# A two-layer hybrid attention backbone on one core: the whole program in one scheduling block, ordered by the timeline machine

## The chip, the cores and the metric

The kernel runs on one core of one Trainium2 chip. The metric is device time in microseconds (us) of that core, from the start of the launch to its end. Three runs of the kernel before took 3088.96 us in the median, between 3088.78 and 3089.18.

## The reference: what is computed

1024 latent tokens and 256 context tokens of width 1024 pass through two layers. Each layer normalizes the tokens, applies a shift and a scale computed from a conditioning vector (adaLN), projects them to many heads with one wide weight matrix, mixes them, projects back and adds the result to the tokens. Cut to what matters here:

```
h = rmsnorm(x, g_pre[l]) * (1.0 + scale) + shift          # also for the context tokens
layer 0:  s = q k^T / 8 ; p = softmax(s)                  # 8 heads, two maps per head
          a = p[0] - lam * p[1] ; oa = rmsnorm(a v) ; ua = oa * silu(gate)
          ub = bb * short_conv(bc * bh) * silu(bg)         # 8 groups of 128 channels
layer 1:  16 heads of 2-D neighbourhood attention (NA) plus dense attention to the context
          4 heads of gated linear attention (GLA), forward and backward
x = x + gate * rmsnorm(u @ w_out[l], g_post[l])
```

All is float32; every product of two matrices is computed as three passes over values split in a high and a low part.

## The kernel before, in words

TensorE (PE) is given nearly all the work that counts. A projection is cut into units: one 1024 x 128 block of a weight matrix is loaded (`wraw`), split into `whi` by ScalarE (ACT, L243) and `wlo` by GpSimd (POOL, L244), and multiplied with the tokens `hA`/`hB` in three chunks of 512, 512 and 256 tokens. One chunk is 24 matmuls into one tile `pj` in PSUM (L437); there are two such tiles (`ps_pj`, bufs=2). Whatever reads a `pj` tile sets when the next chunk but one may start.

Layer 0 goes head by head (`diff_head`, L563). A head has ten steps of 128 query rows (`units`, L640): eight against all 1280 keys, the last two (context queries) against 256 keys. A step computes scores into the single PSUM tile `S` (L589) for map 1, then map 0; VectorE (DVE) takes the row maximum (L591), ACT the exponential `p` (L593), DVE joins the two maps (L599), PE transposes the result (`atr`, L611), ACT and DVE split it into `ath` and `atl` (L614, L615), and after every second step PE multiplies it with the values (`av`, L625). At the end of a head ACT squares the result (L628), PE sums it (`ms`, L635, in the same PSUM slot as `S`), ACT takes logarithm and exponential for the reciprocal root (L309, L310, each with a table load), DVE refines it with three operations (L311 to L313) and multiplies (L637).

Between these dependent steps the program runs projection units of other heads and of the convolution as filler: `ws.run(n)` asks for n more units of the list in `units0`, `ws.until` for all up to a name. The keys of a head go through `rope` (L511), which copies a `pj` tile with ACT (L516) into a buffer of the pool tag `p0`. That tag has two buffers, which the probabilities `p0`, the reciprocal root `rs` and the `ropex` tiles share.

Layer 1 runs GLA heads and then eight pairs of NA heads (`na`, L1403) in the same manner: scores `NS` (L1435, two halves of one PSUM tile), bias and minimum on DVE (L1439), exponential on ACT, scaling on POOL (L1443), transposes `ntr` (L1484), a split into `pth` and `ptl` by ACT and DVE (L1493, L1494), and the product with the values `nav` (L1461). Projections `pj` of the next pair are the filler.

The order of the instructions on each engine comes from the tile framework's scheduler. It takes the program as traced, with its dependencies and priorities, and fixes the queue of every engine before the launch; on the chip each engine runs its queue strictly in that order and waits where an operand isn't ready. Before, the program stands in no block, and the default machine orders it. The last stage (L909) is a `manual_schedule` block, written in its final order.

Of the kernel before, what the change touches and what calls it, by code (L numbers as in the profile page):

```python
# [40 lines left out]
class Stream:  # L41
# [39 lines left out]
    def run(self, n):  # L81
        for _ in range(n):
            if not self.step():
                return
# [15 lines left out]
class Kernel:  # L100
# [6 lines left out]
        return (ctx or self.ctx).enter_context(self.tc.tile_pool(name=name, bufs=bufs, **kw))  # L107

    def run(self):
        self.setup()  # L110
        with ExitStack() as es:
            self.hp = self.pool("hp", ctx=es)
            rope_es, out_es = ExitStack(), ExitStack()
            self.start(rope_es)
            conv_es = self.layer0(rope_es)
            self.layer1(self.out0(conv_es, out_es), out_es)
            with ExitStack() as es2:
                self.out1(es2)
# [1493 lines left out]
```

## Time and profile before

| what | value |
|---|---|
| median of 3 runs | 3088.96 us |
| the profiled execution | 3089.97 us |
| its span | 3087.9 us |
| PE busy | 2935.2 us, 95% |
| DVE, ACT, POOL busy | 1910.7, 1503.5, 1027.9 us |
| mean granted TensorE clock | 0.991 |

Outside the span lie 2.1 us of the profiled execution. PE is idle for 152.7 us of the span; the stretches in which it idles are found with the table of windows, and what it waits for with the list of waits. A row of the waits gives who waited for whom, the us in total, the times and the longest. A row of the timeline gives the start, the time, the engine, the line, and what is written from what; brackets at its end give the idle time before it and who ended it.

### The profile page before, as it was taken

The page shows a single profiled execution, that of the slowest core. Times are in us where ns is not written, and L with a number is a line of the kernel's source. Part 1 is how long each engine was busy: PE and PEld are TensorE (multiplying, and loading weights), DVE is VectorE, ACT ScalarE, POOL GpSimd, SP SyncE. Part 2 cuts the span into 40 slices and gives each one's busy share as a digit, 9 for nine tenths or more (in the row PEclk, how much of TensorE's full clock was granted, in tenths as well). Part 3 has the DMA queues.
Part 4 walks back from the last instruction along what each step waited for, and adds up shares of the span by engine and source line. Part 5 has one row for each costly group of instructions (what it writes and reads, how often), then busy time and mean ns, then how long its engine had stood idle before and what let it go on. Part 6 is the DMA issues. An engine that isn't in the chain of part 4 may idle for free. (4 is left out here: it accounts for less than half of the span.)

```text
span 3087.9 us, 42515 instructions
## 1 busy us (share of the span) xinstructions
PE 2935.2 (95%) x16244; PEld 2439.3 (79%) x16244; DVE 1910.7 (62%) x3272; ACT 1503.5 (49%) x2761; POOL 1027.9 (33%) x813
## 2 busy tenths in 40 slices
PE   6999999999999999999999898989899999999898
PEld 4888888888888887888877777777778888887686
DVE  5675757575665757564244778685836666667723
ACT  4554535353544445453344555555535555556522
POOL 3212131313021211205233334342435555556622
PEclk9999999999999999999999999999999999999999
DMA  6111110211110211115342112111131111113323
GB/s 227 35 45 48 49 52 28 65 35 58 35 59 28 65 35 48 45 42 208 109 150 76 45 39 69 55 43 58 55 95 36 47 44 44 43 44 99 118 76 123
DMA packets 236982, 206.59 MB, mean 67 GB/s; under 512 B 43591, under 2 KB 194538, under 8 KB 236778
## 3 DMA queue, kind: packets, MB, share of 16 engines
q1 hardware_dynamic: 236778, 203.87, 21.2%
q8 instruction: 128, 2.10, 0.3%
q14 instruction: 76, 0.62, 0.1%
HBM read 168.17 MB, written 35.67 MB: 66 GB/s over the span
## 5 line engine op out<-in xcount | busy, mean ns | idle before, releaser
L244 POOL TENSOR_TENSOR wlo<-wraw,whi 128x1024 fp32r<-128x1024 f32 x149 | 367.0, 2463 | 1097.3 <-ACT whi L243 1017.0
L437 PE MATMUL pj<-hBh,whi 128*128 128x512 f32 (+1 forms) x1712 | 383.3, 353 | 6.2 <-ACT hBh L355 4.8
L437 PE MATMUL pj<-hBl,whi 128*128 128x512 f32 (+1 forms) x1712 | 369.1, 347 | 0.9 <-DVE hBl L356 0.9
L437 PE MATMUL pj<-hBh,wlo 128*128 128x512 f32 (+1 forms) x1712 | 352.1, 344 | 0.0
L243 ACT CAST whi<-wraw 128x1024 fp32r<-128x1024 f32 x176 | 184.5, 1048 | 321.3 <-PE ops L753 193.7
L437 PEld LDWEIGHTS pj<-hBl,whi 128*128 128x128 f32 x1712 | 278.0, 191 | 35.9 <-DVE hBl L356 1.1
L437 PEld LDWEIGHTS pj<-hBh,wlo 128*128 128x128 f32 x1712 | 277.2, 190 | 36.8
L437 PEld LDWEIGHTS pj<-hBh,whi 128*128 128x128 f32 x1712 | 273.2, 190 | 40.8 <-ACT hBh L355 5.4
L437 PE MATMUL pj<-hAh,whi 128*128 128x512 f32 x968 | 280.5, 410 | 14.6 <-ACT ropex L516 13.0
L437 PE MATMUL pj<-hAl,whi 128*128 128x512 f32 x968 | 255.4, 395 | 0.0
L591 DVE TENSOR_REDUCE st<-S 128x1 f32<-128x1280 f32 (+1 forms) x160 | 203.9, 1274 | 79.2 <-PE S L589 79.2
L437 PE MATMUL pj<-hAh,wlo 128*128 128x512 f32 x968 | 249.9, 393 | 0.0
L1443 POOL TENSOR_TENSOR np<-np,nst 128x640 f32<-128x640 f32 x128 | 166.5, 1304 | 193.1 <-DVE nst L1442 161.0
L593 ACT ACTIVATE p<-S,st 128x1280 f32<-128x1280 f32 (+1 forms) x160 | 186.1, 1163 | 81.9 <-DVE st L591 80.4
L437 PEld LDWEIGHTS pj<-hAh,wlo 128*128 128x128 f32 x968 | 180.2, 188 | 36.3
L437 PEld LDWEIGHTS pj<-hAh,whi 128*128 128x128 f32 x968 | 170.2, 191 | 48.1 <-ACT ropex L516 14.4
L437 PEld LDWEIGHTS pj<-hAl,whi 128*128 128x128 f32 x968 | 178.7, 190 | 34.8
L589 PE MATMUL S<-kst,qd 128*128 128x512 f32 (+1 forms) x832 | 192.1, 360 | 0.3 <-ACT p L593 0.2
L589 PEld LDWEIGHTS S<-kst,qd 128*128 128x128 f32 x832 | 137.2, 188 | 39.9 <-ACT p L593 21.3
L1439 DVE CUSTOM_DVE_ANT_0 np<-NS,nB 128x640 f32<-128x640 f32 x128 | 105.3, 823 | 91.2 <-PE NS L1436 85.5
L614 ACT CAST ath<-atr 128x512 fp32r<-128x512 f32 (+1 forms) x208 | 99.1, 505 | 113.4 <-PE atr L611 112.8
L1494 DVE TENSOR_TENSOR ptl<-ntr,pth 128x512 fp32r<-128x512 f32 (+2 forms) x224 | 117.6, 536 | 49.0 <-ACT pth L1493 45.2
(361 smaller groups left out, 6276.8 us busy)
## 6 DMA issues: line engine op xcount, KB each, us to landing
wraw<-in_ev_w_in_dram SPq DMA_DIRECT2D x64, 512.0 KB, 4.0
wraw<-in_od_w_in_dram SPq DMA_DIRECT2D x56, 512.0 KB, 3.6
wraw<-in_w_out_dram SPq DMA_DIRECT2D x55, 512.0 KB, 3.7
wraw<-in_w_mod_dram SPq DMA_DIRECT2D x48, 512.0 KB, 3.8
sgT<-gt SPq DMA_DIRECT2D x32, 256.0 KB, 2.0
uT<-sg SPq DMA_DIRECT2D x8, 640.0 KB, 4.3
nG<-in_rpbp_dram SPq DMA_DIRECT2D x128, 40.0 KB, 2.3
xt<-in_x_dram SPq DMA_DIRECT2D x8, 512.0 KB, 6.2
```

The costliest lines, as they stand in the source:

```text
L243: nc.scalar.copy(out=hi, in_=u.raw)
L244: (nc.vector if u.lo_eng == "v" else nc.gpsimd).tensor_tensor(out=lo, in0=u.raw, in1=hi.bitcast(F32), op=ALU.subtract)
L437: nc.tensor.matmul(ps[:, 0:tn], lhsT=a[:, k, :], rhs=self.h_at(k, t0, tn)[b], start=n == 0, stop=n == 23)
L589: nc.tensor.matmul(S[:, c0:c0 + tn], lhsT=qd[:, 2 * m + part, P * qt:P * qt + P], rhs=self.kst[m][:, t0:t0 + tn], start=part == 0, stop=pa ...
L591: nc.vector.tensor_reduce(out=st[:, m:m + 1], in_=S[:, 0:n], axis=AX.X, op=ALU.max, negate=True)
L593: nc.scalar.activation(out=p[m][:, 0:n], in_=S[:, 0:n], func=AF.Exp, bias=st[:, m:m + 1], accum_out=st[:, 2 + m:3 + m])
L614: nc.scalar.copy(out=dh, in_=tv)
L1439: nc.vector.tensor_tensor_reduce(out=p, in0=S[:, z0:z0 + 640], in1=bias[2 * i + m][:, c0:c0 + 640], scale=1.0, scalar=3e38, op0=ALU.add, o ...
L1443: nc.gpsimd.tensor_tensor(out=p, in0=p, in1=st[:, 2:3].broadcast_to([P, 640]), op=ALU.mult)
L1494: nc.vector.tensor_tensor(out=lv[:, s:e], in0=tr[:, s:e], in1=hv[:, s:e].bitcast(F32), op=ALU.subtract)
```

## The change

`run` now opens one block around the whole program and asks for the timeline machine; the old body of `run` becomes `work`.

```diff
     def run(self):
+        with self.tc.block(schedule_with_timeline_sim=True):
+            self.work()
+
+    def work(self):
         self.setup()
         with ExitStack() as es:
             self.hp = self.pool("hp", ctx=es)
```

The instructions themselves, their operands and their buffers stay. In the changed file line numbers are higher by 4 and the numbers in names by 1 (S_3147 is S_3148 there). On PE 15726 instructions, on DVE 3242, on ACT 2387, on POOL 818 and on SP 618 are put in an order; the same ones stand in both. The last stage keeps its order.

**The end of a head, on PE.** This is the second head of layer 0, from the last score step against all keys (S_3147) into the two steps of the context queries (S_3214, S_3223). Before:

```order
L589 MATMUL S_3147<-kst0_2106,qd_3004 128x256
L437 MATMUL pj_3180<-hBh_156,wlo_3057 128x512 x7
L437 MATMUL pj_3250<-hBh_156,whi_3056 128x256 x8
L437 MATMUL pj_3250<-hBl_157,whi_3056 128x256 x5
L589 MATMUL S_3214<-kst1_2107,qd_3206 128x256 x2
L437 MATMUL pj_3250<-hBl_157,whi_3056 128x256 x3
L437 MATMUL pj_3250<-hBh_156,wlo_3057 128x256 x8
L271 MATMUL modps_3278<-wraw_2997,sst_804 32x256
L611 MATMUL atr_3231<-ident_73,p0_3155 128x128 x4
L611 MATMUL atr_3238<-ident_73,p0_3155 128x128 x2
L589 MATMUL S_3223<-kst0_2106,qd_3206 128x256 x2
```

and now:

```order
L593 MATMUL S_3148<-kst0_2107,qd_3005 128x256
L593 MATMUL S_3215<-kst1_2108,qd_3207 128x256 x2
L615 MATMUL atr_3232<-ident_74,p0_3156 128x128 x4
L615 MATMUL atr_3239<-ident_74,p0_3156 128x128 x4
L593 MATMUL S_3224<-kst0_2107,qd_3207 128x256 x2
L629 MATMUL av_3284<-ath_3160,vh_2318 128x256
L615 MATMUL atr_3246<-ident_74,p0_3156 128x128 x2
L629 MATMUL av_3284<-atl_3161,vh_2318 128x256
```

The 31 `pj` matmuls that stood between the scores of S_3147 and the transposes of the next step are gone from here, and so are those behind them up to `ms`; they now stand earlier in the head, between the score steps of the other queries. The same holds at the end of all eight heads.

**The boundary between two heads, on ACT.** From the last square of the second head to the first copies of keys of the third. Before:

```order
L628 ACTIVATE qf_2218<-av_3346 128x256
L309 ACT_TABLE_LOAD
L309 ACTIVATE rt_3360<-ms_3355,eps_80 128x1280
L214 ACT_TABLE_LOAD
L214 ACTIVATE csg_3415<-pj_3386 128x512
L310 ACTIVATE rs_3359<-rt_3360 128x1280
L214 ACTIVATE csg_3445<-pj_3420 128x512
L243 CAST whi_3480<-wraw_3372 128x1024
L214 ACTIVATE csg_3475<-pj_3450 128x256
L516 COPY ropex_3513<-pj_3486 128x512
L529 CAST ropex_3513<-ropex_3513 128x512
L516 COPY ropex_3549<-pj_3524 128x512
```

and now:

```order
L632 ACTIVATE qf_2219<-av_3347 128x256
L313 ACT_TABLE_LOAD
L313 ACTIVATE rt_3361<-ms_3356,eps_81 128x1280
L314 ACT_TABLE_LOAD
L314 ACTIVATE rs_3360<-rt_3361 128x1280
L520 COPY ropex_3514<-pj_3487 128x512
L247 CAST whi_3593<-wraw_3385 128x1024
L533 CAST ropex_3514<-ropex_3514 128x512
L520 COPY ropex_3550<-pj_3525 128x512
L520 COPY ropex_3586<-pj_3561 128x256
```

Before, three silu operations on `pj` tiles of the convolution stood among and behind the table loads, and the first `ropex` copy came after them; now that copy follows the exponential directly.

**The same boundary, on PE.** From the last `ms` to the third head's keys (pj_3486, pj_3524 and pj_3560 are its three chunks; pj_3598 is the first chunk of its queries). Before:

```order
L635 MATMUL ms_3355<-qf_2218,onesD_78 128x256
L437 MATMUL pj_3386<-hAh_154,wlo_3369 128x512 x8
L290 MATMUL modtr_3411<-sel_84,modrow_3378 128x2 x2
L437 MATMUL pj_3420<-hBh_156,whi_3368 128x512 x8
L437 MATMUL pj_3420<-hBl_157,whi_3368 128x512 x8
L437 MATMUL pj_3420<-hBh_156,wlo_3369 128x512 x8
L437 MATMUL pj_3450<-hBh_156,whi_3368 128x256 x8
L437 MATMUL pj_3450<-hBl_157,whi_3368 128x256 x8
L437 MATMUL pj_3450<-hBh_156,wlo_3369 128x256 x8
```

and now:

```order
L639 MATMUL ms_3356<-qf_2219,onesD_79 128x256
L441 MATMUL pj_3561<-hBh_157,whi_3381 128x256 x8
L441 MATMUL pj_3561<-hBl_158,whi_3381 128x256 x8
L441 MATMUL pj_3561<-hBh_157,wlo_3382 128x256 x8
L441 MATMUL pj_3599<-hAh_155,whi_3481 128x512 x8
L441 MATMUL pj_3599<-hAl_156,whi_3481 128x512 x8
```

Before, the convolution's chunks pj_3386, pj_3420 and pj_3450 and then all three key chunks followed `ms`. Now the first two key chunks (pj_3487 and pj_3525) stand ahead of `ms`, and the third follows it at once. All seven boundaries of layer 0 look like this, and the end of the eighth head has no `pj` behind `ms` either: projections back (`ops`) follow.

**A stretch of NA, on PE.** The middle of the second pair of heads; `nqd` is a step's query tile, and a step's scores are two half steps of four `NS` matmuls (two lines of 384 and 256 columns, each twice). Before:

```order
L1484 MATMUL ntr_20935<-ident_73,np_20789 128x128
L1484 MATMUL ntr_20935<-ident_73,np_20799 128x128
L437 MATMUL pj_20946<-hBh_12808,whi_20527 128x512 x5
L1461 MATMUL nav_19409<-pth_20911,nv_20054 128x256 x2
L1461 MATMUL nav_19409<-ptl_20912,nv_20054 128x256 x2
L1461 MATMUL nav_19409<-pth_20927,nv_20054 128x256 x2
L1461 MATMUL nav_19409<-ptl_20928,nv_20054 128x256 x2
L437 MATMUL pj_20946<-hBh_12808,whi_20527 128x512 x3
L437 MATMUL pj_20946<-hBl_12809,whi_20527 128x512 x8
L437 MATMUL pj_20946<-hBh_12808,wlo_20528 128x512 x8
L1435 MATMUL NS_19408<-nk1_19747,nqd_20986 128x384
L1436 MATMUL NS_19408<-nk1_19747,nqd_20986 128x256
```

and now:

```order
L1440 MATMUL NS_19409<-nk0_19747,nqd_20781 128x256
L1465 MATMUL nav_19410<-ptl_20743,nv_20055 128x256 x2
L1488 MATMUL ntr_20821<-ident_74,np_20693 128x128
L1488 MATMUL ntr_20821<-ident_74,np_20703 128x128
L1439 MATMUL NS_19409<-nk1_19748,nqd_20883 128x384
L1440 MATMUL NS_19409<-nk1_19748,nqd_20883 128x256
L1439 MATMUL NS_19409<-nk1_19748,nqd_20883 128x384
L1440 MATMUL NS_19409<-nk1_19748,nqd_20883 128x256
L1488 MATMUL ntr_20836<-ident_74,np_20693 128x128
L1488 MATMUL ntr_20836<-ident_74,np_20703 128x128
L1488 MATMUL ntr_20836<-ident_74,np_20693 128x128
L1488 MATMUL ntr_20836<-ident_74,np_20703 128x128
```

Before, `pj` matmuls (5 to 30 of them) stood behind every half step or every second one throughout. Now seven half steps, from the first of nqd_20781 to the first of nqd_21096, follow each other with transposes and values alone between them, and longer runs of up to 43 `pj` matmuls stand in the rest of the pair. There is one such stretch of seven in each of the eight pairs.

**At the start, on SP.** The loads of the last seven blocks of modulation weights (of 16) and of `rowsB` have moved back: 22 loads of 512 KB stood ahead of `rowsB`, now 33 do, among them the rest of `x`, the context, cos and sin and the first projection weights.

**In GLA, on PE.** The projections between the first and the last `gl` matmul (L1137) of a head fall from 36.1 us to 31.7 us in the second to fourth head, and rise from 33.0 to 36.3 us in the first (the matmuls counted in the orders, at about 0.22 us for 512 columns and 0.12 us for 256, as they follow each other in the trace).

## Rows read from the trace of the kernel before

**Rows 1.** The page, span and busy time by engine.

```profile
span 3087.9 us, 42515 instructions
...
PE 2935.2 (95%) x16244; PEld 2439.3 (79%) x16244; DVE 1910.7 (62%) x3272; ACT 1503.5 (49%) x2761; POOL 1027.9 (33%) x813
```

**Rows 2.** Windows of four stages: busy time of each engine.

```profile
core 0: us, PE busy (x) PEld busy (x) DVE busy (x) ACT busy (x) POOL busy (x), PEclk, DMA share, GB/s
0.00:50.00 50.00, 28.30 (x210) 18.00 (x211) 21.57 (x68) 20.73 (x33) 10.12 (x14) 0.90 0.96 338
...
100.00:600.00 500.00, 495.90 (x2842) 414.76 (x2841) 316.82 (x507) 236.58 (x381) 102.77 (x54) 1.00 0.15 46
...
1700.00:2300.00 600.00, 548.39 (x3036) 451.24 (x3035) 428.26 (x680) 323.93 (x685) 227.80 (x182) 1.00 0.19 58
2300.00:2800.00 500.00, 481.77 (x2830) 410.20 (x2830) 331.20 (x706) 273.49 (x581) 277.34 (x297) 1.00 0.17 44
```

**Rows 3.** Waits of PE: us in total, times, longest.

```profile
PE gl L1137 <- DVE QL L1132: 28.6, 20, 1.8
PE pj L437 <- ACT ropex L516: 13.0, 7, 5.3
```

**Rows 4.** Timeline of PE at the end of the second head.

```profile
365.68 1.77 PE L437 MATMUL pj<-hBh,wlo 128*128 128x512 f32 x7
367.29 1.12 PE L437 MATMUL pj<-hBh,whi 128*128 128x256 f32 x8
...
368.88 0.50 PE L589 MATMUL S<-kst,qd 128*128 128x256 f32 x2
...
371.18 0.88 PE L611 MATMUL atr<-ident,p 128*128 128x128 f32 x6
...
384.95 0.63 PE L635 MATMUL ms<-qf,onesD 128*128 128x256 f32 x2
```

**Rows 5.** Timeline of DVE in the same stretch.

```profile
365.88 1.49 DVE L591 TENSOR_REDUCE st<-S 128x1 f32<-128x1280 f32 x1 [0.78 <-PE S L589]
...
369.06 1.55 DVE L599 SCALAR_TENSOR_TENSOR p<-p,st,p 128x1280 f32<-128x1280 f32 x1
...
374.43 0.69 DVE L615 TENSOR_TENSOR atl<-atr,ath 128x512 fp32r<-128x512 f32 x1 [0.18 <-ACT ath L614]
...
380.20 0.42 DVE L591 TENSOR_REDUCE st<-S 128x1 f32<-128x256 f32 x1 [0.20 <-PE S L589]
...
381.45 0.49 DVE L599 SCALAR_TENSOR_TENSOR p<-p,st,p 128x256 f32<-128x256 f32 x1
```

**Rows 6.** Timeline of ACT in the same stretch.

```profile
367.41 1.33 ACT L593 ACTIVATE p<-S,st 128x1280 f32<-128x1280 f32 x1 [1.18 <-DVE st L591]
...
371.87 0.59 ACT L614 CAST ath<-atr 128x512 fp32r<-128x512 f32 x1 [0.27 <-PE atr L611]
...
380.66 0.48 ACT L593 ACTIVATE p<-S,st 128x256 f32<-128x256 f32 x1
```

**Rows 7.** Timeline of PE at the boundary of the seventh and eighth head.

```profile
1234.68 3.78 PE L437 MATMUL pj<-hAh,whi 128*128 128x512 f32 x8 [5.29 <-ACT ropex L516]
...
1240.33 1.98 PE L437 MATMUL pj<-hAh,wlo 128*128 128x512 f32 x8
```

**Rows 8.** Timeline of ACT at that boundary.

```profile
1217.60 0.38 ACT L628 ACTIVATE qf<-av 128x256 f32<-128x256 f32 x1 [1.42 <-PE av L625]
1218.00 1.28 ACT L309 ACT_TABLE_LOAD   x1
1219.30 1.33 ACT L309 ACTIVATE rt<-ms,eps 128x1280 f32<-128x1280 f32 x1
...
1223.12 0.57 ACT L516 COPY ropex<-pj 128x512 f32<-128x512 f32 x1
...
1234.04 0.59 ACT L516 COPY ropex<-pj 128x512 f32<-128x512 f32 x1 [0.78 <-DVE sg L637]
```

**Rows 9.** Window of one pair of NA, columns as in the windows above.

```profile
2400.00:2466.00 66.00, 64.63 (x390) 55.60 (x390) 43.74 (x95) 38.10 (x82) 38.87 (x43) 1.00 0.15 40
```

## The prediction

> **What bounds the kernel now.** I read the busy times first: PE is busy for 2935.2 of 3087.9 us [rows 1], so the time is PE's work and PE's idle time, here 152.7 us. The instructions stay, so only the idle time can move, and the half clock that follows it. Next the windows: in the heads of layer 0 PE idles 4.1 us in 500; in GLA 51.6 in 600; in NA 18.2 in 500; in the first 50 us 21.7, with the DMA engines 0.96 busy [rows 2]. Then the waits: the largest are GLA's `gl` for a product of DVE, 28.6 us, and `pj` for a `ropex` copy, 13.0 us in 7 waits [rows 3]. In layer 0 PE works 99% of the time already, so a new order has much more to lose there than to win. Last the timelines of the ends of heads, to see how much the cover is worth.
>
> An engine runs its queue in order. So the question for each place is: how long is the chain of other engines between two dependent matmuls, and how much PE work stands between them in the queue? Where the chain is longer, PE idles by the difference.
>
> **The end of a head (8 times).** Take the end of S_3147 as zero; DVE starts its maximum there, at 365.88. Maximum 1.49 and exponential 1.33 bring the next scores into the single `S` slot to 368.88, that is 3.0 [rows 4 to 6]. Today 1.77 + 1.12 us of `pj` and some more cover exactly this [rows 4]; now nothing does. Step by step in the new order: scores of the context step at 3.0; the join of the maps runs 369.06 to 370.61 [rows 5], so transposes start at 4.9 and take about 0.9 us (0.88 for six [rows 4]); the split takes 0.59 on ACT and 0.69 on DVE [rows 5, 6], and frees a transpose buffer at about 7.1; 30 value matmuls at 0.12 us (eight of 256 columns in 1.12 us less the overlap [rows 4]) reach 10.7; transposes and scores among them 11.3; then the last context step: maximum 0.42, exponential 0.48, join 0.49 [rows 5, 6] with a hop of about 0.2 each, 13.6; transposes and the smaller split about 1.3 (estimated from 0.59 + 0.69 for twice the columns, plus two hops), 14.9; six value matmuls 0.7, the square 0.38 [rows 8] and its hop, and `ms`: 16.5 us. PE's own work in this is about 7.7 us (36 value matmuls 4.3, 14 transposes 1.5, scores 0.9, `ms` 1.0). Idle: 8.8 us per head, 8 x 8.8 = 70. From the other side, PE today reaches the last `ms` at 384.95, through a queue full of other work [rows 4], so the chain is no longer than 19.1 us, and the idle time at most 11.4 per head, 91. At least the bare 3.0 us of the first step stays, 24. I take 70.
>
> **The boundary (7 times).** Now pj_3561 comes right behind `ms` and needs the PSUM tile of pj_3487, and pj_3599 that of pj_3525. Both are freed by `ropex` copies, and ACT's queue has these behind table load, logarithm, load, exponential. Today's trace shows this chain once, at the seventh boundary, where a head has only three convolution units: square 1217.60, first copy 1223.12 to 1223.69, second copy 1234.04, because it waits for the buffer of `rs`, which DVE's refinement and product hold [rows 8]; PE resumes at 1234.68 [rows 7]. DVE's queue at all the new boundaries has the same eight operations in the same order. So: from `ms` (1218.5) to 1223.7 idle 5.2; the third chunk, 24 matmuls of 256 columns, 2.9 [rows 4], to 1226.6; idle to 1234.7, 8.1. Together 13.3, 7 x 13.3 = 93. Today the first part is hidden behind chunks of the convolution. The bound above is the whole 17.1 us less 2.9, 99; below, if the copies get their buffers at the end of the exponential and the refinement holds nothing, 5.2 x 7 = 36. I take 93.
>
> **The clock.** After the 5.29 us of idle time the eight matmuls took 3.78 us instead of 1.98 [rows 7]: a start at 1.2 GHz costs 1.8 us. One such start per boundary, 7 x 1.8 = 13, zero to twice that (one in the end of the head too). Away go today's 13.0 us of waits for `ropex` [rows 3] and the 1.8. Layer 0: 70 + 93 + 13 - 15 = +161.
>
> On this the Trainium skill, "TensorE: Matmul & The Clock Gate", section "HAM oscillation — how this bites in real kernels", says that where a wait recurs between short bursts the way back to the full clock is paid at each recurrence and not once. [Rows 7] agree for one wait; by the rule the ends of heads and the NA stretches below would pay too. That is the second rival.
>
> A second page speaks on the boundary: "ScalarE: Activation LUTs", section "What ACT_TABLE_LOAD costs", puts a switch at about 2.66 us, a load plus a drain. Here the load starts at 1218.00 and the logarithm at 1219.30, so the switch costs 1.3 us [rows 8]. By the page two loads would add 2.7 us to each boundary, 19 in all; the row decides.
>
> **NA (8 pairs).** A pair takes 66.0 us, of which DVE works 43.74 [rows 9]: 2.73 us for each of its 16 half steps. A stretch of seven half steps without `pj` thus holds 19.1 us of DVE work, while PE has about 9.7 us between its first and last scores (28 score matmuls at 0.14, 30 transposes at 0.1, 23 value matmuls at 0.12). If DVE set the pace, PE would idle 9.4 us per pair, 75 in all. Some of DVE's share (splits of the next pair's keys and queries, which come with `pj`) falls outside the stretch: I take 7. Today's idle time of a pair is 66.0 - 64.6 = 1.4 [rows 9], 2.4 on the mean of the stage [rows 2]. 8 x (7 - 2) = +40; below, all of today's idle time goes, -19; above +75 and, less today's, +60.
>
> **GLA (4 heads).** Between the first and the last `gl` three heads lose 36.1 - 31.7 = 4.4 us of cover, one wins 3.3. This stretch idles already, waiting for DVE [rows 3], so the cover lost is idle time won: 3 x 4.4 - 3.3 = 10. The `go`, `gu` and `gob` groups, which share one buffer, now stand closer together; I add 2 per head, 8, by the longest wait in the list, 1.8 [rows 3]. +18. Ends: -52 if all of today's idle time went [rows 2], +45 if each head lost as much again as it idles today (13).
>
> **The start.** `rowsB` and the last modulation weights have 11 more loads of 512 KB ahead of them: 5.77 MB at 338 GB/s [rows 2] are 17 us. Some comes back, as those loads are needed by the same work a little later and PE idles there anyway (21.7 us). +8, between 0 and 17. The stages between the two layers and after NA move both ways: 0, ± 10.
>
> **Sum.** 161 + 40 + 18 + 8 = +227. Against the profiled execution's 3089.97 us that is 3317; the median of the runs is 1.0 below it, so 3316; I say 3315 us.
>
> **Rivals.**
> 1. *Only part of layer 0 shows.* The price of the end of a head and of the boundary were added, but ACT's and DVE's chains could overlap better than my walk, and GLA and NA could absorb their changes with buffers (probabilities in NA have five). Then the boundary alone stays: 93 + 13 - 15 = 91, with the bare 24 of the context step, +115: about 3205. For it: the stretch in NA follows a rich one. Against: `S` has one slot and the order of PE is strict.
> 2. *The clock stays low.* If PE's clock falls in every end of a head and every NA stretch, the 7.7 us of work at the end of a head double where the chain does not hide them (half, +4 x 8) and NA pays 1.8 once per pair and again in GLA (+22): +54, about 3370. For it: [rows 7]. Against: in these places PE waits in pieces of 1 to 3 us with work between.
> 3. *Faster.* The timeline machine knows durations, and could have placed GLA's `gl` behind its products and the NA scores behind their queries: 28.6 us go [rows 3], NA's 19 too, and the ends of heads cost nothing if projections reach them in time. 3089 - 48 = 3041. It decides from the point where at least 3.0 us of PE work stand before each next score; at the end of every head the order has none. Against it too: GLA's cover fell.
> 4. *No change.* The queues differ but the same waits decide. 3089, within 0.2% (6.2 us, about what a measurement can tell from no change). The queue of PE in layer 0 rules it out, unless gains elsewhere match.
>
> **Chances.** Forecast 0.57, rival 1 0.18, rival 2 0.17, rival 3 0.05, rival 4 0.03. Faster by over 0.2%: 0.05; within: 0.03; slower: 0.92. The forecast's own range, from the ends that are not excluded by more than one term at a time, is 3240 to 3370. For 8 in 10 I go to the middles of rivals 1 and 2 and a little above, 3200 to 3400.
>
> **What would show it.** In layer 0 a head takes about 22 us longer; behind the last `S` of 1280 keys PE waits 3 us for `p`; at each boundary two waits for `ropex`, about 5 and 8 us, 7 times, where one was; half clock behind the second. In NA, waits of about 1 us at `NS` for the minimum of DVE, bunched once a pair. In GLA the wait for QL stays. I am wrong if the waits for `ropex` total under 40 us, if the scores of the context steps start without a wait, or if PE's idle time in NA is below 25 us.

## The result: slower by 9.6%, and the profile after

The changed kernel took 3386.95 us in the median of 3 runs (3382.07 to 3389.03), before 3088.96. The ratio is 1.0962, with a 95% interval of 1.0937 to 1.0987. The forecast was 3315 us, between 3200 and 3400: the sign and the range held, the size was 72 us short.

The page of the kernel after, span and busy time by engine [rows 1]:

```profile
span 3385.1 us, 42625 instructions
...
PE 3019.4 (89%) x16244; PEld 2555.7 (75%) x16244; DVE 1925.5 (57%) x3272; ACT 1493.6 (44%) x2761; POOL 1021.4 (30%) x813
```

The span is 297.2 us longer. PE, which runs the same matmuls, is busy for 84.2 us more (3019.4 against 2935.2) and idle for 213.0 us more (365.7 against 152.7). So more than a quarter of the loss isn't waiting: it is the same matmuls, taking longer. The mean granted clock fell from 0.991 to 0.949.

Where it went is seen with windows whose borders are events of the program: first scores, last `ms`, last `ops` of layer 0, first and last `gl`, first and last `NS`. The kernel before; after the span comes the stretch's length, then the busy time of PE, and so on as in [rows 2]:

```profile
107.00:1379.10 1272.10, 1258.14 (x7225) 1050.85 (x7224) 807.14 (x1293) 611.34 (x989) 248.46 (x130) 1.00 0.15 46
1379.10:1633.30 254.20, 249.25 (x1129) 206.26 (x1128) 102.99 (x149) 99.21 (x149) 97.37 (x57) 0.99 0.43 145
1633.30:1718.90 85.60, 79.44 (x403) 65.95 (x401) 42.23 (x80) 42.23 (x71) 26.99 (x18) 0.96 0.22 67
1718.90:2219.30 500.40, 451.67 (x2530) 371.35 (x2530) 384.49 (x597) 284.25 (x592) 197.67 (x154) 1.00 0.17 52
2219.30:2316.60 97.30, 92.69 (x472) 76.11 (x470) 37.90 (x73) 35.52 (x85) 34.03 (x35) 1.00 0.31 90
2316.60:2903.40 586.80, 557.29 (x3275) 473.12 (x3276) 411.24 (x855) 335.55 (x711) 335.05 (x348) 0.99 0.19 53
```

And the kernel after:

```profile
108.30:1624.70 1516.40, 1353.82 (x7425) 1151.02 (x7425) 861.83 (x1318) 621.10 (x1013) 276.16 (x143) 0.93 0.14 43
1624.70:1869.00 244.30, 226.35 (x1007) 186.11 (x1006) 77.42 (x132) 85.11 (x129) 73.49 (x45) 0.96 0.38 123
1869.00:1941.30 72.30, 70.54 (x362) 58.83 (x361) 39.63 (x81) 42.35 (x67) 21.43 (x17) 1.00 0.27 80
1941.30:2466.00 524.70, 474.37 (x2591) 406.68 (x2590) 379.45 (x598) 283.04 (x596) 192.18 (x154) 0.95 0.17 50
2466.00:2582.10 116.10, 101.38 (x472) 83.44 (x472) 40.18 (x74) 35.53 (x86) 36.65 (x39) 0.93 0.29 82
2582.10:3207.30 625.20, 560.59 (x3276) 487.24 (x3275) 409.77 (x856) 335.90 (x712) 340.45 (x346) 0.98 0.18 51
```

Layer 0 grew by 244.3 us. Some of that is work that moved into it: it has 200 more matmul instructions, and the start and the stage behind it 79 and 122 fewer. The three together (0 to 1869.00 against 0 to 1633.30) grew by 235.7: PE is idle for 170.8 more (9.2 in the start, 148.6 in layer 0, 13.0 in the stage behind) and busy for 64.9 more. GLA with the stages on both sides (713.1 us to 2582.10, against 683.3) grew by 29.8, of which 7.3 idle; the clock in GLA is 0.95 where it was 1.00. NA and the end grew by 31.7, 34.8 more idle and 3.1 less busy.

What PE waits for after, as in [rows 3] (the largest totals, then three that are named below):

```profile
PE pj L441 <- ACT ropex L520: 78.4, 14, 6.5
PE S L593 <- ACT p L597: 32.5, 18, 3.0
PE NS L1439 <- DVE nst L1443: 20.8, 25, 1.9
...
PE pj L441 <- DVE csg L219: 17.5, 12, 2.6
PE ops L757 <- ACT uh L742: 16.3, 1, 16.3
...
PE gl L1141 <- DVE QL L1136: 9.7, 5, 2.7
```

The waits for `ropex` went from 13.0 us in 7 to 78.4 in 14. The GLA wait for QL, which was to stay, went down from 28.6 to 9.7; others took its place there, as the stage's idle time went up by 1.6.

The end of the second head and the boundary behind it, on PE (before: [rows 4, 7]):

```profile
448.18 0.50 PE L593 MATMUL S<-kst,qd 128*128 128x256 f32 x2 [3.04 <-ACT p L597]
449.96 1.97 PE L615 MATMUL atr<-ident,p 128*128 128x128 f32 x8 [1.29 <-DVE p L603]
...
459.49 1.98 PE L639 MATMUL ms<-qf,onesD 128*128 128x512 f32 x4 [1.11 <-ACT p L597]
...
463.95 0.70 PE L639 MATMUL ms<-qf,onesD 128*128 128x256 f32 x2 [0.47 <-ACT qf L632]
469.65 2.07 PE L441 MATMUL pj<-hBh,whi 128*128 128x256 f32 x8 [4.99 <-ACT ropex L520]
...
472.95 1.12 PE L441 MATMUL pj<-hBh,wlo 128*128 128x256 f32 x8
480.59 3.78 PE L441 MATMUL pj<-hAh,whi 128*128 128x512 f32 x8 [6.51 <-ACT ropex L520]
484.17 2.97 PE L441 MATMUL pj<-hAl,whi 128*128 128x512 f32 x8
486.98 2.00 PE L441 MATMUL pj<-hAh,wlo 128*128 128x512 f32 x8
488.81 1.98 PE L441 MATMUL pj<-hBh,whi 128*128 128x512 f32 x8
```

The waits stand where the walk put them: 3.04 us for `p` before the scores of the context step, 1.29 for the join, 1.11 and 0.47 at `ms`, then 4.99 and 6.51 for the two `ropex` copies. Behind them matmuls run at half speed: eight of 512 columns take 3.78 us where eight take 2.00 at 486.98. The granted clock, in windows of 3 us, behind a wait of 2.62 us for `csg` (to 417.64) earlier in the head, at the end of the head and at the boundary:

```profile
418.00:421.00 3.00, 3.00 (x17) 3.00 (x16) 2.90 (x4) 0.00 (x0) 1.17 (x1) 0.50 0.26 93
451.00:454.00 3.00, 3.00 (x15) 2.80 (x14) 2.46 (x7) 2.30 (x6) 0.00 (x0) 0.50 0.02 5
469.65:472.65 3.00, 3.00 (x14) 3.00 (x15) 3.00 (x5) 0.00 (x0) 1.21 (x1) 0.51 0.00 0
481.00:484.00 3.00, 3.00 (x8) 2.32 (x8) 2.92 (x6) 0.78 (x2) 1.07 (x1) 0.50 0.97 276
...
487.00:490.00 3.00, 3.00 (x15) 2.47 (x14) 2.49 (x6) 1.01 (x2) 0.00 (x0) 1.00 0.02 5
```

The third column from the end is the clock. It is at its lower level, 0.50 (1.2 GHz), behind the waits of 2.62, 3.04, 4.99 and 6.51 us, the two shorter ones too, and back at 1.00 (2.4 GHz) at the end of the list. Behind the 1.11 us at `ms` it stayed at 1.00.

### The profile page after: what moved, and what is told of

It is laid out like the page before. It is cut to its first block, busy times and chain, and to the rows that moved or that the text cites. A ratio compares the mean times of both kernels' runs of the same rounds, so it can differ in the third digit from the quotient of the medians.

```text
span 3385.1 us, 42625 instructions
## 1 busy us (share of the span) xinstructions
PE 3019.4 (89%) x16244; PEld 2555.7 (75%) x16244; DVE 1925.5 (57%) x3272; ACT 1493.6 (44%) x2761; POOL 1021.4 (30%) x813
## 5 line engine op out<-in xcount | busy, mean ns | idle before, releaser
L248 POOL TENSOR_TENSOR wlo<-wraw,whi 128x1024 fp32r<-128x1024 f32 x149 | 380.9, 2557 | 995.2 <-ACT whi L247 724.0
L441 PE MATMUL pj<-hBh,wlo 128*128 128x512 f32 (+1 forms) x1712 | 378.3, 350 | 0.0
L441 PEld LDWEIGHTS pj<-hBh,whi 128*128 128x128 f32 x1712 | 291.6, 199 | 110.5 <-ACT ropex L520 37.8
L441 PEld LDWEIGHTS pj<-hBl,whi 128*128 128x128 f32 x1712 | 289.4, 199 | 40.1 <-DVE hBl L360 2.6
L441 PEld LDWEIGHTS pj<-hBh,wlo 128*128 128x128 f32 x1712 | 277.2, 192 | 32.5
L441 PE MATMUL pj<-hAh,wlo 128*128 128x512 f32 x968 | 259.9, 395 | 0.0
L441 PEld LDWEIGHTS pj<-hAh,whi 128*128 128x128 f32 x968 | 186.4, 203 | 95.8 <-ACT ropex L520 44.9
L593 PE MATMUL S<-kst,qd 128*128 128x512 f32 (+1 forms) x832 | 196.2, 367 | 37.1 <-ACT p L597 32.5
L441 PEld LDWEIGHTS pj<-hAl,whi 128*128 128x128 f32 x968 | 187.1, 195 | 39.8
L593 PEld LDWEIGHTS S<-kst,qd 128*128 128x128 f32 x832 | 145.8, 198 | 63.2 <-ACT p L597 38.1
L619 DVE TENSOR_TENSOR atl<-atr,ath 128x512 fp32r<-128x512 f32 (+1 forms) x208 | 117.9, 583 | 129.8 <-ACT ath L618 128.4
L524 POOL TENSOR_TENSOR ropex<-ropex,sin 128x512 f32<-128x512 f32 x32 | 57.7, 1802 | 423.0 <-DVE ropex L522 423.0
```

The source lines that it names most:

```text
L248: (nc.vector if u.lo_eng == "v" else nc.gpsimd).tensor_tensor(out=lo, in0=u.raw, in1=hi.bitcast(F32), op=ALU.subtract)
L441: nc.tensor.matmul(ps[:, 0:tn], lhsT=a[:, k, :], rhs=self.h_at(k, t0, tn)[b], start=n == 0, stop=n == 23)
L524: nc.gpsimd.tensor_tensor(out=s, in0=s, in1=self.sin[:, t0:t0 + tn], op=ALU.mult)
L593: nc.tensor.matmul(S[:, c0:c0 + tn], lhsT=qd[:, 2 * m + part, P * qt:P * qt + P], rhs=self.kst[m][:, t0:t0 + tn], start=part == 0, stop=pa ...
L619: nc.vector.tensor_tensor(out=atl[:, g0:g0 + gn, P * qt:P * qt + P], in0=tv, in1=dh.bitcast(F32), op=ALU.subtract)
```

## The experiments

In several of them a queue is held to an order. That is done with edges between instructions of one engine that cost no semaphore; where only some queues are held, the scheduler lays the others anew around them, so such a kernel is not simply one engine of one kernel with the rest of the other. The diffs show the lines that matter, with lists of instructions and long expressions put in words. The times are compared with 3386.95 us for the changed kernel and 3088.96 for the kernel before; ratios are to the kernel before.

**The block alone.** The block, with the default machine.

```diff
-        with self.tc.block(schedule_with_timeline_sim=True):
+        with self.tc.block():
```

> The block alone, with the default machine. Theory (the new order of the queues costs the 298 us, the block nothing): 3089 us within 0.2%, PE's idle time 153 us. Rival (the block itself costs, by other waits at its borders or in its code): clearly above 3095 us, and then that much less of the 298 us is the order's.

Measured: 3089.25 us, ratio 1.0001 (0.9992 to 1.0011). The queues of PE, POOL and SP are the same, instruction for instruction, as those of the kernel before. The block costs nothing that can be measured; the loss comes with the timeline machine's order.

**PE's order in layer 0, held to before.**

```diff
         with self.tc.block(schedule_with_timeline_sim=True):
             self.work()
+            self.pin()     # for a, b in neighbours of the list: add_manual_dep(b, a, NoSync)
...
+PIN = (PE's queue of before, from the start to the last ms of layer 0)
```

> The timeline machine, but PE's queue from the start to the last ms of layer 0 held to the order of before by edges that cost no semaphore; the other engines and the rest of the program are the timeline machine's. Theory (PE's order in layer 0 carries about 218 us of waits and half clock, 27.2 us more for each of 8 heads, and the 16.3 us wait of ops for uh behind them): 3387 - 218 - 16 = 3150 us, from 3125 to 3180. Rival (the orders of ACT and DVE cost as much as PE's): over 3230 us. Rival (NA and GLA were hurt by what layer 0 did before them): under 3110 us.

Measured: 3188.13 us (ratio 1.0328, 1.0311 to 1.0345), 199 us off the changed kernel and a little above the range. Layer 0 took 1304.4 us, idle 30.3. The rest of the loss stands elsewhere: GLA 523.8 and NA 620.1 us, close to the changed kernel's 524.7 and 625.2. So NA and GLA aren't hurt by what layer 0 did before them. In layer 0, which is 32 us above before, 12.2 us of waits for `csg` and 9.2 for `p` remain:

```profile
PE pj L452 <- DVE csg L230: 12.2, 6, 2.1
...
PE S L604 <- ACT p L608: 9.2, 8, 1.4
```

**The other way round.** The default machine, with PE's queue in layer 0 held to the timeline machine's order.

```diff
             with ExitStack() as es2:
                 self.out1(es2)
+        self.pin()
...
+PIN = (PE's queue of the changed kernel, from the start to the last ms of layer 0)
```

> The other way round: the kernel before with its default machine, and PE's queue from the start to the last ms of layer 0 held to the timeline machine's order. Theory (PE's order in layer 0 is enough by itself for the loss there): layer 0 takes 1490 to 1520 us instead of 1272, the next stage 10 less, GLA and NA stay at 500 and 587: 3310 us, from 3285 to 3335. Rival (the default machine's order of ACT and DVE, laid around that, hides much of it): under 3250 us.

Measured: 3346.3 us (ratio 1.0827, 1.0811 to 1.0844), above the range. Layer 0 took 1539.4 us, GLA 501.1 and NA 586.5, as before the change. PE's order is enough for the loss of layer 0, and with the queues that the default machine laid around it the stage is 23 us longer than in the changed kernel (waits for `csg` are 25.7 us instead of 17.5); the same two waits lead:

```profile
PE pj L448 <- ACT ropex L527: 78.0, 14, 6.6
PE S L600 <- ACT p L604: 32.3, 14, 3.9
...
PE pj L448 <- DVE csg L226: 25.7, 12, 3.5
```

**Keys behind `ms`.** One edge per boundary.

```diff
+            self.gates[f"k{h + 1}/0"] = mm     # the last ms matmul of head h
...
+                if n == 0:
+                    self.gate(mm, name)        # first matmul of chunk 0 of k{h+1}: issue after it
```

> The timeline machine with one edge per boundary: the next head's first key chunk may stand on PE only behind the last ms. Theory of the boundary: both waits for ropex (78.4 us in 14) shrink, since two chunks of 5.2 us each and a third of 2.9 us now stand before the copy that waits for rs; 0 + about 3 us are left of 4.99 + 6.51, and most of the half clock behind them (3.4 us) goes: 7 x 11 to 12 = 77 to 84, 3387 - 80 = 3307 us, from 3290 to 3325. The ends of heads keep their 3.04 us wait. Rival (what PE doesn't wait for at the boundary it waits for elsewhere in the head, since the filler is the same): 3370 us or more.

Measured: 3316.17 us (ratio 1.0733, 1.071 to 1.0756), 71 less than the changed kernel and in the range. The order is then `ms`, three key chunks, queries, and of the waits for `ropex` 0.6 us are left in each boundary. But waits for `p` grew from 32.5 to 45.1 us: the two chunks that now stand behind `ms` no longer cover steps before it, so part of the rival is true.

**Filler for the end of heads too.**

```diff
+                if (qp, qt, m) == (3, 1, 0):   # last scores against all keys
+                    self.gates[<last convolution unit of head h> + "/0"] = mm
```

> As the kernel with late keys, and the last convolution unit of each head may stand on PE only behind the last scores against all keys: 13.3 us of filler go into the end of heads 1 to 6, as the order shows; heads 7 and 8 are not reached. Theory: the waits at the end of a head (3.04 + 1.29 + 1.11 + 0.47 = 5.9 us) and the half clock there (about 3 us) go in six heads, 6 x 9 = 54 more: 3307 - 54 = 3253 us, from 3230 to 3275. Rival (the earlier steps lose the filler and wait instead): within 15 us of the kernel with late keys alone.

Measured: 3296.5 us (ratio 1.0674, 1.0654 to 1.0694), 20 less than late keys alone: between the two. In the heads that the edge reaches, the end lost its 3.04 us wait, but a step earlier in the head got one of the same length, and others short ones:

```profile
PE S L601 <- ACT p L607: 41.4, 37, 3.0
...
PE atr L625 <- DVE atl L629: 20.5, 16, 2.6
```

The rival has most of it. Filler is a fixed amount per head, and here an edge that brought it to one chain took much of it from another. The order of before, which leaves 0.2 us of waits for `p` in the whole of layer 0, isn't reached by one or two edges.

**`rs` in another buffer.** In the changed kernel and in the kernel before.

```diff
-        r = self.rstd(ap.tile([P, TOK], F32, name="rs", tag="p0", bufs=2), ...
+        r = self.rstd(self.ap2.tile([P, 10, 256], F32R, name="rs", tag="ath").rearrange("p a b -> p (a b)").bitcast(F32)[:, 0:TOK], ...
```

> The timeline machine, and the reciprocal root rs put into the buffer of ath, so that it no longer holds one of the two buffers that the ropex copies need; the machine plans anew with that. Theory (the second wait at the boundary, 6.51 us, is for the buffer of rs and nothing else): both copies follow the exponential, the wait and the 3.4 us of half clock behind it go, 7 x 9.9 = 69: 3318 us, from 3295 to 3340. Rival (filler is what lacks; a wait removed here comes back elsewhere in the head): 3355 us or more.

Measured: 3263.35 us (ratio 1.056, 1.0546 to 1.0574), 124 less than the changed kernel, below the range. All waits for `ropex` are gone, both of the boundary and not the second alone, and the machine used the free buffers to stand the third key chunk and the first query chunk between the last `ms` matmuls; both `ropex` copies now stand on ACT ahead of the table loads. That the second copy waits for the buffer of `rs` is read from the changed kernel's trace, where it starts behind `sg`, the last operation to read `rs` (row 479.95 below). This run is in line with that, but it doesn't separate the buffer from the new order that came with it.

> The kernel before, with rs in the buffer of ath in the same way. Theory: its waits of pj for ropex (13.0 us in 7) go, and with the longest the 1.8 us at half clock: 3089 - 15 = 3074 us, from 3070 to 3079. Rival (the copies then wait for ACT's or DVE's queue): 3085 us or more.

Measured: 3088.85 us, ratio 0.9996 (0.9988 to 1.0005): no change. The theory fell here. The wait of 5.29 us [rows 7] is gone from its place, and one of 4.16 us stands 13 us later, at the first chunk of the next projection (1247.62), for another `ropex` copy; of the 13.0 us in 7 waits [rows 3], 12.0 in 8 are left. The six others, of 1.3 us each, are untouched, so that buffer isn't their cause.

**The clock at the boundary.** Matmuls that nobody reads, put into both waits.

```diff
+        if k2:                                           # the third key chunk
+            self.gates[name] = self.burn(36, hi, "warm1")       # behind ms, before the chunk
...
+            self.gates[f"q{h + 1}/0"] = self.burn(54, hi, "warm2")   # behind the chunk, before the queries
```

> The timeline machine, with matmuls that nobody reads put into both waits of each boundary (36 behind the last ms, 54 behind the third key chunk, 256 columns each, into the free half of av; about 0.12 us each, 4.3 and 6.4 us of waits of 4.99 and 6.51). They add work and take nothing away. Theory of the clock: PE comes out of the boundary at 2.4 GHz, the next 24 matmuls take 6.0 us instead of 8.4: 7 x 2.4 to 3.4 = 17 to 24 us less, 3387 - 20 = 3367 us, from 3358 to 3377. Rival (the half clock there is hidden behind the waits that follow): 3382 us or more; above 3395 us if the added matmuls themselves come late.

Measured: 3354.12 us (ratio 1.0855, 1.0839 to 1.0872), 33 less and just below the range. 630 added matmuls made the kernel faster. The dummies run until the query chunk may start, which then runs at full clock:

```profile
459.75 0.70 PE L661 MATMUL ms<-qf,onesD 128*128 128x256 f32 x2 [0.47 <-ACT qf L654]
...
468.42 6.64 PE L437 MATMUL av<-hAh,whi 128*128 128x256 f32 x54
474.90 2.00 PE L458 MATMUL pj<-hAh,whi 128*128 128x512 f32 x8
...
480.37 1.98 PE L458 MATMUL pj<-hBh,whi 128*128 128x512 f32 x8
```

24 matmuls take 5.5 us (474.90 to 480.37) instead of 8.2 (480.59 to 488.81): 2.7 per boundary, 19 in all, and this is the clock. In the same places the way from the last `ms` to the queries is 1.5 us shorter (459.75 to 474.90, against 463.95 to 480.59), 10 in all, and this is not the clock. The machine planned the other queues anew, and POOL's split `wlo` came later. In the changed kernel it runs beside a DVE addition that stands between `rs` and `sg`; first the changed kernel, then the one with the dummies:

```profile
474.34 3.63 POOL L248 TENSOR_TENSOR wlo<-wraw,whi 128x1024 fp32r<-128x1024 f32 x1 [0.52 <-ACT whi L247]
475.69 2.82 DVE L525 TENSOR_TENSOR ropex<-ropex 128x512 f32<-128x512 f32 x1
```
```profile
471.51 0.68 DVE L547 TENSOR_TENSOR ropex<-ropex 128x512 f32<-128x512 f32 x1
```

The addition is 2.1 us shorter, and so the second copy comes 2.1 us sooner; the last dummies use 0.7 of it. Where the last 4 us come from is open.

**NA, and the other queues.** PE's order of before in NA alone.

```diff
+PIN = (PE's queue of before, from the first to the last NS)
```

> The timeline machine with PE's queue held to the order of before between the first and the last scores of NA alone. Theory (the stretches of seven half steps without projections make DVE set the pace): NA's stage goes from 625 back to about 590 us, its idle time from 65 to about 32, and the sum to 3387 - 35 = 3352 us, from 3342 to 3362. Rival (NA waits for DVE because DVE's own queue changed): 3375 us or more.

Measured: 3397.98 us (ratio 1.1, 1.0984 to 1.1017): NA took 639.0 us instead of 625. The theory of NA fell in this form. PE has its filler back where it was, and in NA it now waits most for `nu`, from a DVE queue planned by the timeline machine:

```profile
PE nav L1476 <- DVE nu L1482: 31.5, 42, 1.4
PE NS L1450 <- DVE nqd L1439: 12.3, 7, 3.1
```

Then PE's whole queue, PE's and DVE's, and DVE's alone.

```diff
+PIN = [(PE's queue of before), (DVE's queue of before)]    # both, or one of them
```

> The timeline machine with PE's whole queue, up to the last stage, held to the order of before; the other engines' queues are the timeline machine's. Holding layer 0 alone left 3188 us: GLA, NA and the stretch between them still 58 to 60 us above before, layer 0 32, the start 11, and 14 to 16 less in the two stages between. Theory (PE's order carries the cost): the 58 us go and about 40 stay from ACT's and DVE's order: 3130 us, from 3110 to 3150. Rival (in GLA and NA it is the order of DVE and ACT): 3165 us or more.

Measured: 3200.75 us (ratio 1.036, 1.0346 to 1.0374). GLA 526.1 us, NA 640.4: in the rival's range, and 13 us slower than with PE held in layer 0 alone.

> The timeline machine with the queues of PE and of DVE, up to the last stage, held to the order of before; ACT, POOL and SP are the timeline machine's. With PE alone held it was 3200.75 us: layer 0 27 above before, GLA 26, NA 53, the start 12. Theory (in GLA and NA, and in the rest of layer 0, DVE's queue carries the cost): only the start stays, 3090 + 12 = 3102 us, from 3090 to 3120. Rival (ACT's queue carries it): 3165 us or more.

Measured: 3168.64 us (ratio 1.0255, 1.024 to 1.0271). Layer 0 is back at 1275.7 us: with PE's and DVE's queues held, nearly the whole loss there is gone. The time is in the rival's range, but that ACT's queue makes it is not shown. GLA took 515.8, NA 627.7, with 27.1 us of waits of `ntr` for POOL's `np` that neither kernel had in this size.

> The timeline machine with DVE's queue alone held to the order of before; PE's is free. Theory (DVE's queue sets when the two pj tiles come free, and so how early the filler may run): layer 0 comes down as well, the sum to 3200 us or less. Rival (DVE's queue matters in GLA and NA alone, PE runs its filler as early as before): 3387 - 26 - 38 = 3323 us, 3300 to 3345.

Measured: 3590.6 us (ratio 1.1617, 1.1597 to 1.1636), slower than every other kernel here: neither theory. GLA took 617.7 and NA 719.7 us. Here a queue planned for one order, laid against another, cost more than either order; so these kernels don't tell which single queue costs the 38 us of NA, and that stays open.

## Why the prediction was right, and where its size was off

**The step that was mis-sized is the clock.** The idle time was forecast at +216 us (layer 0 70 + 93 - 13 = 150, NA 40, GLA 18, start 8), and 213.0 were measured. That this is so close is in part luck. Start and layer 0 with the stage behind had 170.8 where the forecast had 158, GLA with its neighbours 7.3 for 18, NA with the end 34.8 for 40. And inside layer 0 both large terms were forecast too high: the ends of heads idle 50.6 us and not 70, the boundaries 78.4 and not 93. Waits that the walk hadn't, those of 17.5 us for `csg` the largest, made up for them.

The clock was forecast at 13 - 1.8 = 11 us, one start at 1.2 GHz per boundary, and PE's busy time grew by 84.2. In a head like the one shown the clock falls four times: after 2.62 us of waiting for `csg`, after 3.04 and its successors at the end of the head, and after both waits of the boundary. The walk counted one start at 1.2 GHz per boundary, by [rows 7], and none behind waits of 1 to 3 us. That one start was also priced too low: 1.8 us is the first eight matmuls alone, and all 24 lose 2.7 (8.2 instead of 5.5).

The rest is rival 2 (3370 us, 0.17), and the time lies nearer to it than to the forecast: what it priced at 54 was 73 (84.2 - 11). It had the places right in part: PE's busy time grew by 64.9 us up to the end of layer 0 and by 22.5 in GLA and its neighbours, but not in NA and the end (-3.1). That a clock kept up gives time back is shown by the dummies, and at the boundary alone; at the ends of heads and in GLA the granted clock is all there is to show it. The Trainium skill, "TensorE: Matmul & The Clock Gate", section "HAM oscillation — how this bites in real kernels", has it that the way back to the full clock is paid at each recurrence of a wait. The windows above agree.

Not all of the 84 us lengthens the span. From the last scores (445.14) to the last `ms` (463.95) it is 18.8 us, where the walk had 16.5. PE waits 5.9 of them, not 8.8, and works 12.9, not 7.7: of the 5.2 us of slower and added work (a few `modtr` among it), 2.9 went into the wait and 2.3 onto the end.

**The end of a head.** The 3.0 us for `p` is there, eight times (2.87 to 3.04). At the ends of heads and the boundaries together it is PE's order that makes the idle time: layer 0 idles 162.6 us in the changed kernel and 30.3 with PE's order of before in it; it idles 14.0 us in the kernel before and 181.9 with PE's new order in it.

**The boundary.** Forecast 5.2 + 8.1 = 13.3 us; measured 4.99 + 6.51 = 11.5. The chain of the seventh boundary [rows 8] repeats row by row: from the square to the second copy 16.4 us (1217.60 to 1234.04), now 16.4 (463.52 to 479.95). Of the 1.8 us less of idle time, 1.5 are the third chunk, which ran into the second wait at half the clock: 24 matmuls to 474.07 are 4.4 us, forecast 2.9. The walk took the chain as a whole and so also took over something that needn't be in it: 2.1 us of the second wait are the DVE addition beside POOL's `wlo`. It takes 2.82 us in all seven boundaries now, and took 2.82 at the boundary of [rows 8]. The chain on ACT, kernel after:

```profile
463.52 0.38 ACT L632 ACTIVATE qf<-av 128x256 f32<-128x256 f32 x1 [1.41 <-PE av L629]
463.92 1.28 ACT L313 ACT_TABLE_LOAD   x1
465.21 1.33 ACT L313 ACTIVATE rt<-ms,eps 128x1280 f32<-128x1280 f32 x1
...
469.03 0.57 ACT L520 COPY ropex<-pj 128x512 f32<-128x512 f32 x1
...
479.95 0.58 ACT L520 COPY ropex<-pj 128x512 f32<-128x512 f32 x1 [0.78 <-DVE sg L641]
```

The table load takes 1.3 us here too, as in [rows 8].

**What was missed in layer 0.** 17.5 us in 12 waits in six heads, for `csg`: PE needs a `pj` tile that DVE has not yet read. And 16.3 us once, behind the eighth head, where `ops` waits for `uh`: that the order has no `pj` behind the last `ms` there was known, but the forecast's sum has no term for it.

**GLA.** Forecast 18 us of more idle time. There is 1.6 more in the stage and 7.3 with its neighbours, so the cover that was counted wasn't missed. But the waits are others, and longer ones: the 20 waits for QL of 1.8 us at most became 5 with 2.7 at most, and waits of up to 3.2 us for other tiles came. The clock, which held at 1.00, fell to 0.95.

**NA.** Forecast 40, measured 38.4, 35.1 of it idle. The place is as forecast: in one pair the stretch of seven half steps goes from 2778 to 2797, with DVE busy for 16.6 of 19 us and waits of 2.15, 1.53, 0.45, 0.42 and 0.42 us in it:

```profile
2778.00:2797.00 19.00, 14.56 (x86) 12.47 (x86) 16.60 (x37) 12.67 (x28) 11.18 (x13) 0.91 0.11 18
```
```profile
2778.55 0.48 PE L1465 MATMUL nav<-pth,nv 128*128 128x256 f32 x2 [2.15 <-DVE nu L1471]
...
2787.36 0.46 PE L1439 MATMUL NS<-nk,nqd 128*128 128x384 f32 x1 [1.53 <-DVE nst L1443]
```

The largest of them is for `nu`, not for the minimum. That PE without filler is the cause wasn't confirmed: with PE's order of before the stage was slower still. The size was right, the reason is not shown.

**The start.** Forecast +8 of idle time, measured +9.2; the stretch itself is only 1.3 us longer, with 79 fewer matmuls in it. With PE's order held, the start took 118.0 us, 11 more than before, 5.1 of them idle; that the later loads cost this is likely but not separated from the other queues.

No version here beats the kernel before. The one candidate that came out of the forecast's walk, `rs` in another buffer, made no difference to it.

## What to carry to other kernels

Where one engine is busy 99% of a stage, its filler work is a fixed budget against fixed chains: walk each chain, add up what stands beside it in the queue, and any order that spends the budget early is paid at the end. Price every wait of two to three us on TensorE twice, once as the wait and once as the clock behind it, in each of its recurrences; the sum of idle time came out within 2% here, partly by luck, and the time was still 72 us short. And don't take one engine's order out of a plan without a run: PE's order of before in layer 0 gave back 199 of 298 us, but DVE's alone made the slowest kernel of all.

## What the runs showed of the hardware that was not expected

The forecast counted on the lower clock behind one long wait per boundary. Behind a wait of 2.62 us it was at 0.50 too, and eight matmuls of 256 columns took 1.82 us, where eight take 1.12 at full clock [rows 4]. That was no exception: of the 23 waits of 2.5 to 3.2 us in the kernel after, 22 have a mean granted clock below 0.9 in the 3 us behind them, and of the 43 of 0.8 to 1.5 us 13 have. And 630 more matmuls of 0.12 us, whose results nobody reads, put into the waits, took 33 us off the kernel, 19 of them by the clock.

The DVE addition took 2.82 us beside POOL's `wlo` and 0.68 without it. In the kernel after, seven of its 32 executions take 2.82 us, the seven that run beside `wlo` for over 2 us, and the other 25 take 0.67 to 0.69.
